# Seven products for eight: the feed-forward blocks of a decoder layer on one core, by Strassen's method

## The chip, the core and the metric

The kernel is written for one Trainium2 chip and runs on one of its cores, as a single program. The metric is the device time of one execution in microseconds (us), lower is better; several executions are timed and their median is given. One further execution was recorded by the hardware profiler; all views of the profile below are of that one. In them PE is TensorE (matmuls), PEld its weight loads, DVE VectorE, ACT ScalarE, POOL GpSimd, and SP the engine whose queue issues the transfers. L199 is line 199 of the kernel.

## What is computed

One decoder layer on 512 tokens of width 1024 in float32. The parts that the change touches are the two SwiGLU feed-forward blocks (FFNs), hidden width 2816, at the head of the layer and after the mixers:

```python
def swiglu(x, w_gate, w_up, w_down):
    return (jax.nn.silu(x @ w_gate) * (x @ w_up)) @ w_down

h = x + 0.5 * swiglu(rms_norm(h, g_ffn1), w_ffn1_gate, w_ffn1_up, w_ffn1_down)
u = rms_norm(h, g_mix);  z = u @ w_in        # convolution branch, q, k, v, gates
...                                          # conv module, dilated attention, merge
h = h + (g_a * y_conv + g_b * y_attn) @ w_mix_out
h = h + 0.5 * swiglu(rms_norm(h, g_ffn2), w_ffn2_gate, w_ffn2_up, w_ffn2_down)
h = h + sigmoid(rms_norm(h, g_ple) @ w_ple_gate) * (p @ w_ple_proj)
y = rms_norm(h, g_final)
```

## The kernel before

Activations lie transposed: a tile is 128 features by 512 tokens (`T`, 73 of them), so the width is KD = 8 tiles and the hidden width KF = 22. A product runs as three matmuls in a format that the tensor engine takes at full rate: every operand is split into a high part, which ACT rounds off with a copy, and a low part, the difference, which DVE (or POOL) subtracts. `mm3` (L198 to L201) multiplies high by high, high by low and low by high into one bank of PSUM. Activations are split by `split` (L209), weights by `split_one` (L161): ACT writes `wh` (L177), DVE writes `wl` (L182); for the slabs of the mixer named in `POOLED`, POOL writes `wl` in two halves (L180).

Weights arrive as slabs of 128 partitions by up to 1024 columns, in the order that `slab_order` writes out. `slab` (L186), called when PE comes to a slab, issues the loads up to three slabs ahead of the splits and the splits two slabs ahead of the use; RAW = 3 tiles hold slabs as loaded and SPLIT = 3 pairs hold them split. All loads go through the SP queue.

`ffn` (L338) loops over the 22 hidden row blocks: a unit of 24 matmuls of 512 columns for gate into bank `pg`, one for up into `pu`. Then DVE multiplies by the tokens' 1/rms (R), ACT takes silu, DVE multiplies, and the hidden tile is split. After that it loops over the 8 output blocks of down: 66 matmuls each into bank `pd`, then DVE adds half of it to the residual, and `into` (L389) splits the new residual for the next stage and adds its square to the next norm. In FFN 1 the 31 DVE steps that make the rotary tables (`tables`) are handed out two at a time by `background` between the units of down.

`begin` (L241) loads x and the first two slabs in pieces and splits them; `Norm.by_token` and `on_all` produce 1/rms while PE goes on with products that don't need it yet. The mixers follow (L463 on): gated convolution inputs, head slots of attention with the convolution in PSUM by DVE beside them, merge gates, output products. FFN 2 and the per-layer embedding end the layer; there PE runs matmuls of 256 columns, since the last stage is done in two halves of the tokens (`pg<-xsh,pgh`).

Of the kernel before, what the change touches and what calls it, by code (L numbers as in the profile page):

```python
# [38 lines left out]
C_M0, C_M1, C_M2, C_FREQ = 0, 256, 768, 1280  # L39
NCST = 1281  # L40
MAGIC = float(0x5F3759DF)

# 2 KiB tiles of activations
NT = 73
SLAB = 1024          # columns of a weight slab
# weight slabs in flight: as loaded, and split
RAW = 3
SPLIT = 3
AHEAD = 2            # slabs split ahead of their use
# slabs whose second part GpSimd takes, while VectorE works on the convolution in PSUM  # L50
POOLED = ("win", "v", "ao")
# steps of the depthwise convolution beside a unit of each kind
# [23 lines left out]

def slab_order():
    out = []
    for m in range(KF):
        out += [("g1", m), ("u1", m)]  # L80
    out += [("d1", m, j) for m in range(KD) for j in range(3)]
# [11 lines left out]
    for m in range(KF):  # L93
        out += [("g2", m), ("u2", m)]
    out += [("d2", m, j) for m in range(KD) for j in range(3)]
    out += [("pT",), ("pp", 0), ("pp", 1)]
    out += [("pg", m) for m in range(KD)]
    return out
# [3 lines left out]
def block_kernel(ctx: ExitStack, tc: tile.TileContext, a, out):  # L102
# [18 lines left out]
    def bank(n="ps"):  # L121
        return psum.tile([P, S], F32, name=name(n), tag="ps", bufs=6)
# [4 lines left out]
    # ---- weights: loaded ahead, split into two parts that the tensor engine takes exactly  # L127
    order = slab_order()
    state = {"load": 0, "split": 0, "use": 0}
    raws, halves = {}, {}  # L130

    def source(key):
        kind = key[0]
        if kind in ("d1", "d2"):
            lo, hi = ((0, 1024), (1024, 1920), (1920, 2816))[key[2]]
            return a["w_ffn%s_down" % kind[1]][key[1], :, lo:hi]
# [4 lines left out]
        n = {"g1": "w_ffn1_gate", "u1": "w_ffn1_up", "g2": "w_ffn2_gate", "u2": "w_ffn2_up", "win": "w_in",  # L141
             "ao": "w_attn_out", "co": "w_conv_out", "mx": "w_mix_out", "pg": "w_ple_gate", "pp": "w_ple_proj"}[kind]
        return a[n][key[1]]

    def raw_tile():
        return wts.tile([P, SLAB], F32, name=name("wr"), tag="wr", bufs=RAW)

    def split_tiles():
        return (wts.tile([P, SLAB], F32R, name=name("wh"), tag="wh", bufs=SPLIT),
                wts.tile([P, SLAB], F32R, name=name("wl"), tag="wl", bufs=SPLIT))  # L150

    def load_one():
        i = state["load"]
        src = source(order[i])
        w = src.shape[-1]
        r = raw_tile()
        nc.sync.dma_start(r[:, :w], src)
        raws[i] = (r, w)
        state["load"] = i + 1

    def split_one():  # L161
        i = state["split"]
        r, w = raws.pop(i)
        kind = order[i][0]
        if kind == "pg":
            hs, ls = [], []
            for c in range(2):
                z = r[:, c * S:(c + 1) * S]
                h, l = T("pgh", F32R), T("pgl", F32R)
# [5 lines left out]
        else:  # L175
            h, l = split_tiles()
            A.activation(h[:, :w], r[:, :w], AF.Copy)  # L177
# [3 lines left out]
            else:  # L181
                V.tensor_sub(l[:, :w], r[:, :w], h[:, :w].bitcast(F32))  # L182
            halves[i] = (h, l)
        state["split"] = i + 1

    def slab(key):  # L186
# [3 lines left out]
        while state["split"] <= min(i + AHEAD, len(order) - 1):  # L190
            while state["load"] <= state["split"]:
                load_one()
            split_one()
        while state["load"] < min(state["split"] + RAW, len(order)):
            load_one()
        return halves.pop(i)

    def mm3(ps, wh, wl, xh, xl, start, stop):  # L198
        PE.matmul(ps, wh, xh, start=start, stop=False)  # L199
        PE.matmul(ps, wh, xl, start=False, stop=False)  # L200
        PE.matmul(ps, wl, xh, start=False, stop=stop)  # L201

    def unit(ps, key, xs, start=True, stop=True, at=0):
        h, l = slab(key)
        for k, (xh, xl) in enumerate(xs):
            c = slice((at + k) * P, (at + k + 1) * P)
            mm3(ps, h[:, c], l[:, c], xh, xl, start and k == 0, stop and k == len(xs) - 1)
# [13 lines left out]
    # ---- constants, and the first loads  # L221
    gx = const.tile([P, V_DW + S], F32, name="gx")
    gains, x0 = gx[:, :V_DW], gx[:, V_DW:]
    taps = const.tile([P, KD * TAPS], F32, name="taps")
    ident = const.tile([P, P], F32, name="ident")
    cst = const.tile([P, NCST], F32, name="cst")
# [14 lines left out]
    def begin():  # L241
        """The first two slabs and x arrive in pieces, in the order in which they are used."""
        rs_ = [raw_tile() for _ in range(2)]
        hl = [split_tiles() for _ in range(2)]
        x = [x0] + [T("x") for _ in range(KD - 1)]
        xs = []
        cuts = [slice(0, 256), slice(256, 512), slice(512, 1024)]

        def piece(j):
            for i in range(2):  # L250
                nc.sync.dma_start(rs_[i][:, cuts[j]], source(order[i])[:, cuts[j]])

        def part(j):
            c = cuts[j]
            for i in range(2):
# [3 lines left out]
        nc.sync.dma_start(gx, a["gx"])  # L259
# [6 lines left out]
        state["load"] = state["split"] = 2  # L266
        load_one()
        nc.sync.dma_start(cst, a["cst"])
        nc.sync.dma_start(taps, a["taps"])
        for c in range(KD):  # L270
            xs.append(split(x[c], "xs", gain(V_G1, c)))
            if c in (0, 2, 3):
# [4 lines left out]
    class Norm:  # L277
        """The sum of squares over the features, and 1 / rms of every token: by token, and on every partition."""
# [58 lines left out]
    # ---- FFN  # L337
    def ffn(n, xs, norm, resid, after, first=False):  # L338
        R = None
        hid = []  # L340
        late = []

        def finish(pg, pu, tg, tu, gated=False):
            if not gated:
                V.tensor_mul(tg, pg, R)
                A.activation(tg, tg, AF.Silu)
            V.tensor_mul(tu, pu, R)
            V.tensor_mul(tu, tu, tg)  # L348
            hid.append(split(tu, "hid"))

        for m in range(KF):
            pg, pu = bank("pg"), bank("pu")
            tg, tu = T("tg"), T("tu")
            if first and m == 0:
                ga = slab(("g" + n, m))
                for t in resid:
                    norm.add(t)
                norm.flush()
                ua = slab(("u" + n, m))
                for k, (xh, xl) in enumerate(xs):  # L360
                    c = slice(k * P, (k + 1) * P)
                    mm3(pg, ga[0][:, c], ga[1][:, c], xh, xl, k == 0, k == KD - 1)
                    mm3(pu, ua[0][:, c], ua[1][:, c], xh, xl, k == 0, k == KD - 1)
                late.append((pg, pu, tg, tu))
                continue
            unit(pg, ("g" + n, m), xs)
            gated = R is not None
            if gated:
                V.tensor_mul(tg, pg, R)
                A.activation(tg, tg, AF.Silu)  # L370
            else:
                norm.by_token()
            unit(pu, ("u" + n, m), xs)
            if not gated:
                R = norm.on_all()
                for z in late:
                    finish(*z)
                late.clear()
            finish(pg, pu, tg, tu, gated)
        xs.clear()  # L380
        for m in range(KD):
            p = bank("pd")
            for j, (k0, k1) in enumerate(((0, 8), (8, 15), (15, 22))):
                unit(p, ("d" + n, m, j), hid[k0:k1], start=j == 0, stop=j == 2)
                background(2)
            V.scalar_tensor_tensor(resid[m], p, 0.5, resid[m], op0=OP.mult, op1=OP.add)
            after(m)

    def into(v, xs, norm, resid):  # L389
        def after(m):  # L390
# [529 lines left out]
```

## Time and profile before

| | |
|---|---|
| median of 3 runs | 1349.77 us (1349.27 to 1349.83) |
| span of the profiled execution | 1347.4 us |
| PE busy | 1334.2 us, 99% |
| DVE, ACT, POOL busy | 796.8, 499.7, 198.8 us |
| granted clock of TensorE, mean | 0.998 |
| bytes moved | 127.48 MB, 95 GB/s |

The profiled execution's own time beyond its span is not listed; the timed runs lie 1.9 to 2.4 us above the span. A row of a group gives line, engine, operation, what it writes and reads, shapes and count, then the sum busy, the mean duration in ns, and the idle time before it with what ended it. A row of the timeline gives start, duration, engine, line, operation and how many in a row are merged. A row of a stretch gives each engine's busy time, in brackets its instructions, then TensorE's granted clock, the share of the transfer engines and GB/s.

### The profile page before, as it was taken

How to read it: one execution, taken by the hardware profiler on the slowest of the kernel's cores; microseconds unless marked ns; L12 is line 12 of the kernel's file. 1: busy time of each engine (PE TensorE's matmuls, PEld its weight loads, DVE VectorE, ACT ScalarE, POOL GpSimd, SP SyncE). 2: the span in 40 equal slices, each digit the busy share in tenths (PEclk: the TensorE clock that was granted, in tenths of full speed). 3: DMA queues.
4: the chain of work that ended last, by engine and by line, in shares of the span. 5: the costliest groups of instructions: out<-in, count | busy, mean ns of one | idle time of the engine just before them, and what ended most of it. 6: DMA issues, size and time to landing. Idle time of an engine off the chain costs nothing.

```text
span 1347.4 us, 16023 instructions
## 1 busy us (share of the span) xinstructions
PE 1334.2 (99%) x6340; PEld 1127.7 (84%) x6340; DVE 796.8 (59%) x1283; ACT 499.7 (37%) x704; POOL 198.8 (15%) x164
## 2 busy tenths in 40 slices
PE   9999999999999999999999999999999999999997
PEld 7888888888888888989898878888888888888897
DVE  6544444455359887777778957555444444334465
ACT  5322332222332355555563345343222233223353
POOL 0000000000155443333334340000000000000020
PEclk9999999999999999999999999999999999999999
DMA  6222322333322222222222222222223222332321
GB/s 229 94 94 97 106 94 92 101 101 97 104 86 102 79 94 71 86 68 75 67 90 79 95 94 93 95 94 94 94 94 104 100 94 90 102 100 87 108 79 63
DMA packets 37947, 127.48 MB, mean 95 GB/s; under 512 B 4208, under 2 KB 4976, under 8 KB 37872
## 3 DMA queue, kind: packets, MB, share of 16 engines
q1 hardware_dynamic: 37872, 126.46, 27.9%
q8 instruction: 49, 0.80, 0.2%
q14 instruction: 26, 0.21, 0.0%
HBM read 124.35 MB, written 2.10 MB: 94 GB/s over the span
## 4 chain that ended last, share of the span: by engine, by line
PE 96%; DVE 3%; ACT 0%; DMA 0%; issue 0%; SPq 0%; DVEq 0%
PE pg L200 9%; PE pg L201 9%; PE pg L199 9%; PE pd L199 6%; PE pu L199 6%; PE pd L201 6%; PE pd L200 6%; PE pu L200 6%; PE pu L201 6%; PE pq L201 3%; PE pq L199 3%; PE pq L200 3%; PE pv L643 2%; PE pv L644 2%; PE pv L645 2%; PE pb L199 1%
## 5 line engine op out<-in xcount | busy, mean ns | idle before, releaser
L177 ACT ACTIVATE wh<-wr 128x1024 fp32r<-128x1024 f32 (+2 forms) x229 | 232.7, 1018 | 133.7 <-PE pd L200 55.5
L180 POOL TENSOR_TENSOR wl<-wr,wh 128x512 fp32r<-128x512 f32 (+1 forms) x152 | 187.6, 1257 | 621.2 <-ACT wh L177 606.2
L182 DVE TENSOR_TENSOR wl<-wr,wh 128x1024 fp32r<-128x1024 f32 x153 | 183.1, 1197 | 160.4 <-ACT wh L177 159.6
L199 PE MATMUL pg<-xsh,wh 128*128 128x512 f32 x480 | 188.6, 393 | 0.9 <-ACT xsh L217 0.9
L200 PE MATMUL pg<-xsl,wh 128*128 128x512 f32 x480 | 187.1, 390 | 0.3 <-DVE xsl L218 0.3
L201 PE MATMUL pg<-xsh,wl 128*128 128x512 f32 x480 | 187.0, 390 | 0.0
L483 DVE SCALAR_TENSOR_TENSOR acc<-glu,taps,acc 128x511 f32<-128x511 f32 (+14 forms) x240 | 165.0, 732 | 0.0
L199 PE MATMUL pu<-xsh,wh 128*128 128x512 f32 x352 | 137.2, 390 | 0.0
L201 PE MATMUL pu<-xsh,wl 128*128 128x512 f32 x352 | 137.0, 389 | 0.0
L200 PE MATMUL pu<-xsl,wh 128*128 128x512 f32 x352 | 137.0, 389 | 0.0
L199 PE MATMUL pd<-hidh,wh 128*128 128x512 f32 x352 | 136.9, 389 | 0.0
L200 PE MATMUL pd<-hidl,wh 128*128 128x512 f32 x352 | 136.9, 389 | 0.0
L201 PE MATMUL pd<-hidh,wl 128*128 128x512 f32 x352 | 136.9, 389 | 0.0
L199 PEld LDWEIGHTS pg<-xsh,wh 128*128 128x128 f32 x480 | 90.2, 188 | 20.7 <-ACT xsh L217 1.3
L200 PEld LDWEIGHTS pg<-xsl,wh 128*128 128x128 f32 x480 | 90.1, 188 | 20.0 <-DVE xsl L218 1.1
L201 PEld LDWEIGHTS pg<-xsh,wl 128*128 128x128 f32 x480 | 90.0, 188 | 18.9
L214 ACT ACTIVATE hidh<-tu 128x512 fp32r<-128x512 f32 x44 | 27.9, 633 | 188.3 <-DVE tu L348 188.3
L171 POOL TENSOR_TENSOR pgl<-wr,pgh 128x512 fp32r<-128x512 f32 x8 | 10.9, 1365 | 487.2 <-PE pp L201 467.2
L201 PEld LDWEIGHTS pu<-xsh,wl 128*128 128x128 f32 x352 | 66.1, 188 | 13.8
L201 PEld LDWEIGHTS pd<-hidh,wl 128*128 128x128 f32 x352 | 66.1, 188 | 13.8
L200 PEld LDWEIGHTS pu<-xsl,wh 128*128 128x128 f32 x352 | 66.1, 188 | 13.7
L200 PEld LDWEIGHTS pd<-hidl,wh 128*128 128x128 f32 x352 | 66.1, 188 | 13.7
(202 smaller groups left out, 2335.7 us busy)
## 6 DMA issues: line engine op xcount, KB each, us to landing
wr<-in_w_in SPq DMA_DIRECT2D x56, 512.0 KB, 3.2
wr<-in_w_ffn_gate SPq DMA_DIRECT2D x43, 512.0 KB, 3.2
wr<-in_w_ffn_up SPq DMA_DIRECT2D x43, 512.0 KB, 3.2
wr<-in_w_ffn_down SPq DMA_DIRECT2D x32, 448.0 KB, 3.3
wr<-in_w_ffn_down SPq DMA_DIRECT2D x16, 512.0 KB, 3.5
wr<-in_w_v SPq DMA_DIRECT2D x16, 384.0 KB, 2.9
wr<-in_w_conv_out SPq DMA_DIRECT2D x8, 512.0 KB, 3.2
wr<-in_w_mix_out SPq DMA_DIRECT2D x8, 512.0 KB, 3.2
```

Source lines behind the costliest of these rows:

```text
L171: (G if c else V).tensor_sub(l, z, h.bitcast(F32))
L177: A.activation(h[:, :w], r[:, :w], AF.Copy)
L180: G.tensor_sub(l[:, c:c + w // 2], r[:, c:c + w // 2], h[:, c:c + w // 2].bitcast(F32))
L182: V.tensor_sub(l[:, :w], r[:, :w], h[:, :w].bitcast(F32))
L199: PE.matmul(ps, wh, xh, start=start, stop=False)
L200: PE.matmul(ps, wh, xl, start=False, stop=False)
L201: PE.matmul(ps, wl, xh, start=False, stop=stop)
L214: A.activation(hh, src, AF.Copy)
L483: bg.append(lambda acc=acc, g=g, w=w, s=s: V.scalar_tensor_tensor(acc[:, s:], g[:, :S - s], w, acc[:, s:], op0=OP.mult, op1=OP.add))
L643: PE.matmul(pv[b][:, :384], xh, wh[:, c], start=first_, stop=False)
L644: PE.matmul(pv[b][:, :384], xh, wl[:, c], start=False, stop=False)
L645: PE.matmul(pv[b][:, :384], xl, wh[:, c], start=False, stop=last_)
```

## The change

Gate and up, and down, are computed by blocks of two by two: hidden row block m goes with m + 11, feature chunk c with c + 4 (for down, output block m with m + 4), and the 512 tokens are two halves of 256. The product of such a two-by-two weight block with a two-by-two activation block is made of seven products of half size (the variant with shared sums) instead of eight. PE multiplies with 256 columns of tokens.

- The first two pairs of row blocks (`EARLY`) are done whole, while the norm is formed; the others need activations that are already normalised (`normed`).
- Each step (`step`) of gate/up takes one pair of row blocks, both gate and up. Its four weight quarters (128 by 1024) are loaded as two transfers each. POOL makes four sums of quarters (`sum_one`), ACT all high parts, DVE six of the seven low parts and POOL that of T4.
- On the activations, `operands` makes four differences of 256 columns on POOL, then high parts on ACT and low parts on DVE.
- Results come out of three banks: ACT copies three products to SBUF, DVE adds the others to them or to their result; pieces of this work are queued (`job`) and handed out beside the products within budgets per engine (`work`).
- Down has four rounds over 3, 3, 2 and 3 pairs of hidden blocks (`ROUNDS`), each in two halves of the outputs, placed between the gate/up steps by `PLAN`. A round adds its results to the residual: DVE from PSUM, POOL from SBUF (in the last round DVE).
- Tiles are planned anew: 61 of `T`, 16 of 1024 columns (`W`) for weights as loaded, summed and split alike, and for some scores. The residual lies in one constant tile, masks are loaded after FFN 1, and wide scores take two tiles. The mixer's first gates come one unit later and the last products take the feature chunks in the order LAST.

```diff
+PRODUCTS = ("B11", "B21", "T2", "T1", "T3", "B22", "T4")
+EARLY = 2
+ROUNDS = ((0, 1, 2), (3, 4, 5), (6, 7), (8, 9, 10))
+PLAN = (("gu", 2), ("gu", 3), ("dn", 0, 0), ("dn", 0, 1), ("gu", 4), ("gu", 5), ("gu", 6), ("dn", 1, 0), ("dn", 1, 1),
+        ("gu", 7), ("gu", 8), ("gu", 9), ("dn", 2, 0), ("gu", 10), ("dn", 2, 1), ("dn", 3, 0), ("dn", 3, 1))
...
+    def sum_one():
...
+        if q == "B11":
+            r = z(A11)
+            mixed[k, 1] = W("s1")[:, :w]
+            G.tensor_add(mixed[k, 1], z(A21), z(A22))
+        elif q == "B21":
+            r = z(A12)
+            mixed[k, 2] = W("s2")[:, :w]
+            G.tensor_sub(mixed[k, 2], mixed[k, 1], z(A11))
+        elif q == "T2":
+            r = mixed[k, 2]
+            s3 = z(A21, True)
+            G.tensor_sub(s3, z(A11, True), s3)
+            mixed[k, 3] = s3
+        elif q == "T1":
+            r = mixed.pop((k, 1))
+            mixed[k, 4] = W("s4")[:, :w]
+            G.tensor_sub(mixed[k, 4], z(A12, True), mixed.pop((k, 2)))
...
     def split_one():
...
+            A.activation(h, r, AF.Copy)
+            (G if q == "T4" else V).tensor_sub(l, r, h.bitcast(F32))
...
     def slab(key):
...
+        more, sums = (1, 1) if key[0] == "gq" else (MORE, SUMS)
+        for j in range(i + 1, i + AHEAD + sums + 1):
+            ahead("load", load_one, j + 1)
+            ahead("sum", sum_one, j + 1)
+            ahead("split", split_one, min(j, i + AHEAD) + 1)
...
+    def operands(x1, x2, t12, t34):
...
+                A.activation(h, src, AF.Copy)
+                V.tensor_sub(l, src, h.bitcast(F32))
...
+        def sub(o, p_, q_):
+            return lambda: G.tensor_sub(o, p_, q_), 0, 0, 0.7
+        todo = {"T1": sub(t12[:, lo], x1[:, hi], x1[:, lo]), "T3": sub(t34[:, lo], x2[:, hi], x1[:, hi]),
+                "T2": sub(t12[:, hi], x2[:, hi], t12[:, lo]), "T4": sub(t34[:, hi], x2[:, lo], t12[:, hi]),
...
+    def step(n, key, ts, fin, *most, n_bg=0):
+        pa, pe, pd = bank("pa"), bank("pe"), bank("pd")
+        into_ = {"B11": pa, "B21": pe, "T2": pa, "T1": pd, "T3": pa, "B22": pd, "T4": pa}
...
+        for q in PRODUCTS:
+            h, l = slab((n, key, q))
+            ps = into_[q]
+            for i in range(k):
+                th, tl = ts[i][q]
+                for g in range(2):
+                    c = slice((g * k + i) * P, (g * k + i + 1) * P)
+                    mm3(ps[:, g * 256:(g + 1) * 256], h[:, c], l[:, c], th, tl,
+                        q in ("B11", "B21", "T1") and i == g == 0, i == k - 1, True)
+            work(*most)
+            background(n_bg)
+            if q in ("B11", "T2", "T1"):
+                t = kept[q] = T("p")
+                A.activation(t, ps, AF.Copy)
+            else:
+                z, old = {"B21": ((0, 0), "B11"), "T3": ((1, 1), "T1"), "B22": ((0, 1), "T2"), "T4": ((1, 0), None)}[q]
+                fin(*z, kept.get(old), ps)
...
+        def gate_up(j):
...
+                V.tensor_add(t, t, ps)
...
+                job(lambda: A.activation(t[:, lo], t[:, lo], AF.Silu), 0.4)
+                job(lambda: V.scalar_tensor_tensor(dst, t[:, hi], 0.5, t[:, lo], op0=OP.mult, op1=OP.mult), v=0.4)
+            step(n, ("gu", j), xn, out, *((1.0, 0.9, 3) if j < 4 else (0.9, 0.9, 3)), n_bg={4: 2, 5: 1, 6: 2}.get(j, 0))
...
+        def down(r, half):
...
+                add(V, a_, b_, ps)
...
+                elif not last:
+                    for z in rest:
+                        job(lambda z=z: add(G, *z), g=1.3)
...
+            step(n, ("dn", r, half), [ops[j] for j in ROUNDS[r]], out, *((1.3, 1.4, 2) if last else (0.7, 0.7, 2)), n_bg=1)
```

More of the change, by code (lines that the diff above doesn't have):

```diff
@@ L74, with ffn_order @@
 ROUND = 12582912.0
+def ffn_order(n):
+    out = [("gq", n, j, q) for j in range(EARLY) for q in range(4)]
+    for step in PLAN:
+        out += [(n, step, q) for q in PRODUCTS]
+    return out
 def slab_order():
     out = []
-    for m in range(KF):
-        out += [("g1", m), ("u1", m)]
-    out += [("d1", m, j) for m in range(KD) for j in range(3)]
+    out += ffn_order("1")
     for c in range(KD):
@@ L92, in slab_order @@
     out += [("mx", m) for m in range(KD)]
-    for m in range(KF):
-        out += [("g2", m), ("u2", m)]
-    out += [("d2", m, j) for m in range(KD) for j in range(3)]
+    out += ffn_order("2")
     out += [("pT",), ("pp", 0), ("pp", 1)]
@@ L128, in block_kernel, with quarter @@
     order = slab_order()
-    state = {"load": 0, "split": 0, "use": 0}
+    state = {"load": 0, "sum": 0, "split": 0, "use": 0}
     raws, halves = {}, {}
+    def quarter(n, step, q):
+        x_, y = divmod(q, 2)
+        if step[0] == "gu":
+            m = step[1] + x_ * KF // 2
+            return [a["w_ffn%s_%s" % (n, g)][m][:, y * S:(y + 1) * S] for g in ("gate", "up")]
+        js = ROUNDS[step[1]]
+        c = y * KF // 2 + js[0]
+        m = 4 * x_ + 2 * step[2]
+        return [a["w_ffn%s_down" % n][m + i][:, c * P:(c + len(js)) * P] for i in range(2)]
     def source(key):
         kind = key[0]
-        if kind in ("d1", "d2"):
-            lo, hi = ((0, 1024), (1024, 1920), (1920, 2816))[key[2]]
-            return a["w_ffn%s_down" % kind[1]][key[1], :, lo:hi]
         if kind == "v":
@@ L152, in load_one @@
+    quarters, mixed = {}, {}
     def load_one():
         i = state["load"]
[L154 to L158, printed above, removed]
-        state["load"] = i + 1
+        key = order[i]
+        q = product(key)
+        if key[0] == "gq":
+            raws[i] = fetch(*quarter(key[1], ("gu", key[2]), key[3]))
+        elif q is None:
+            raws[i] = fetch(source(key))
+        elif q == "B11":
+            for z in (A21, A22, A11):
+                quarters[key[:2], z] = fetch(*quarter(key[0], key[1], z))
+        elif q == "B21":
+            quarters[key[:2], A12] = fetch(*quarter(key[0], key[1], A12))
+        state["load"] = i + 1
@@ L161, in split_one @@
     def split_one():
         i = state["split"]
[L163 to L166, printed above, removed]
+        r, q, kind = raws.pop(i), product(order[i]), order[i][0]
+        if q is not None:
+            w = r.shape[-1]
+            h, l = W("wh", F32R)[:, :w], W("wl", F32R)[:, :w]
+            A.activation(h, r, AF.Copy)
+            (G if q == "T4" else V).tensor_sub(l, r, h.bitcast(F32))
+            halves[i] = h, l
+        elif kind == "pg":
+            hs, ls, low = [], [], W("wl", F32R)
@@ L167, in split_one @@
             for c in range(2):
                 z = r[:, c * S:(c + 1) * S]
-                h, l = T("pgh", F32R), T("pgl", F32R)
+                h, l = T("pgh", F32R), low[:, c * S:(c + 1) * S]
                 A.activation(h, z, AF.Copy)
@@ L181, in split_one, with ahead @@
             else:
-                V.tensor_sub(l[:, :w], r[:, :w], h[:, :w].bitcast(F32))
+                V.tensor_sub(l, r, h.bitcast(F32))
             halves[i] = (h, l)
         state["split"] = i + 1
+    def ahead(what, one, to):
+        while state[what] < min(to, len(order)):
+            one()
     def slab(key):
@@ L189, in slab, with mm3, unit @@
         state["use"] = i + 1
[L190 to L195, printed above, removed]
-        return halves.pop(i)
[L198 to L203, printed above, removed]
-        h, l = slab(key)
-        for k, (xh, xl) in enumerate(xs):
-            c = slice((at + k) * P, (at + k + 1) * P)
-            mm3(ps, h[:, c], l[:, c], xh, xl, start and k == 0, stop and k == len(xs) - 1)
+        more, sums = (1, 1) if key[0] == "gq" else (MORE, SUMS)
[3 more added lines that the diff above has]
+            ahead("split", split_one, min(j, i + AHEAD) + 1)
+        ahead("load", load_one, i + AHEAD + RAW + 1)
+        if product(order[min(i + AHEAD + RAW, len(order) - 1)]):
+            ahead("load", load_one, i + AHEAD + RAW + more + 1)
+        return halves.pop(i)
+    def mm3(ps, wh, wl, xh, xl, start, stop, part=False):
+        PE.matmul(ps, wh, xh, start=start, stop=False, skip_group_check=part)
+        PE.matmul(ps, wh, xl, start=False, stop=False, skip_group_check=part)
+        PE.matmul(ps, wl, xh, start=False, stop=stop, skip_group_check=part)
+    def unit(ps, key, xs, ks=range(KD), beside={}):
+        h, l = slab(key)
+        for k in ks:
+            if k in beside:
+                beside[k]()
+            c = slice(k * P, (k + 1) * P)
+            mm3(ps, h[:, c], l[:, c], xs[k][0], xs[k][1], k == ks[0], k == ks[-1])
     def split(src, n, scale=None, w=S):
@@ L335, in on_all @@
             return R
[L338 to L352, printed above, removed]
-            tg, tu = T("tg"), T("tu")
[L354 to L357, printed above, removed]
-                norm.flush()
[L359 to L387, printed above, removed]
@@ L389, in into, with job, work @@
-    def into(v, xs, norm, resid):
-        def after(m):
-            xs.append(split(resid[m], "xs", gain(v, m)))
-            norm.add(resid[m])
-            if m == KD - 1:
-                norm.flush()
-        return after
+    jobs = []
+    def job(f, a_=0.0, v=0.0, g=0.0):
+        jobs.append((f, (a_, v, g)))
+    def work(*most):
+        sum_ = [0.0] * 3
+        while jobs:
+            sum_ = [x_ + y for x_, y in zip(sum_, jobs[0][1])]
+            if any(x_ > y for x_, y in zip(sum_, most)):
+                break
+            jobs.pop(0)[0]()
@@ L397, in block_kernel, with into, first_, second @@
+    def into(v, xs, norm, resid):
+        seen = []
+        def first_(m):
+            xs[m] = split(resid[m], "xs", gain(v, m))
+        def second(m):
+            norm.add(resid[m])
+            seen.append(m)
+            if len(seen) == KD:
+                norm.flush()
+        return first_, second
     bg = []
@@ L451, in tables @@
         bg.append(end)
-    x, xs = begin()
     norm = Norm()
+    x, xs = begin(norm)
+    norm.flush()
     h = x
-    us, unorm = [], Norm()
-    nxt = into(V_GM, us, unorm, h)
-    def after1(m):
-        nxt(m)
-        if m == 0:
-            tables()
-    ffn("1", xs, norm, h, after1, first=True)
+    us, unorm = [None] * KD, Norm()
+    ffn("1", xs, norm, h, into(V_GM, us, unorm, h))
     background(len(bg))
+    masks = []
+    for g in range(NG):
+        masks.append(T("mask"))
+        nc.sync.dma_start(masks[g][:, :C_M[g + 1] - C_M[g]], a["cst"][:, C_M[g]:C_M[g + 1]])
     conv = {}
```

330 lines of the change are left out of this document (259 added, 71 removed).

## The prediction, made before the changed kernel ran

> **What bounds the kernel now.** I read the page first: span, busy shares, then the chain that ended last.
>
> ```profile
> span 1347.4 us, 16023 instructions
> PE 1334.2 (99%) x6340; PEld 1127.7 (84%) x6340; DVE 796.8 (59%) x1283; ACT 499.7 (37%) x704; POOL 198.8 (15%) x164
> PE 96%; DVE 3%; ACT 0%; DMA 0%; issue 0%; SPq 0%; DVEq 0%
> ```
>
> The chain is 96% PE, so the time is the sum of the matmuls' spacings plus a few gaps. A matmul's listed duration (390 ns for 512 columns) overlaps its neighbours, so I take spacings from the timeline: where both feed-forward blocks (FFNs) begin and end, and a stretch of 256-column matmuls in the last stage, whose form is the one that the change uses.
>
> ```profile
> 4.87 0.50 PE L199 MATMUL pg<-xsh,wh 128*128 128x512 f32 x1
> 368.03 0.39 PE L199 MATMUL pb<-xsh,wh 128*128 128x512 f32 x1
> ...
> 911.35 0.39 PE L199 MATMUL pg<-xsh,wh 128*128 128x512 f32 x1
> ...
> 916.95 0.79 PE ss L307 x8
> 923.35 0.86 PE R L328 x2
> ...
> 1272.26 0.39 PE L199 MATMUL pp<-wh,wh 128*128 128x512 f32 x1
> ...
> 1326.96 0.28 PE L200 MATMUL pg<-xsl,pgh 128*128 128x256 f32 x1
> 1334.99 0.28 PE L201 MATMUL pg<-xsh,pgl 128*128 128x256 f32 x1
> ```
>
> FFN 1 takes 363.2 us (368.03 - 4.87), FFN 2 360.9 (1272.26 - 911.35). Each holds 1584 matmuls of 512 columns (22 x 16 x 3 for gate and up, 8 x 22 x 3 for down); less the 1.65 us of norm work in FFN 2 (ss and R), that is 0.227 us each. The 256-column stretch holds 67 spacings in 8.03 us: 0.120 us each. So half a matmul costs 0.53 of a whole one, with its own weight load each time.
>
> Next the view by stretches, one from inside FFN 2, for who is free beside PE.
>
> ```profile
> core 0: us, PE busy (x) PEld busy (x) DVE busy (x) ACT busy (x) POOL busy (x), PEclk, DMA share, GB/s
> 1000.00:1100.00 100.00, 100.00 (x443) 82.78 (x442) 48.36 (x56) 28.64 (x37) 0.00 (x0) 1.00 0.29 100
> ```
>
> In the FFNs POOL does nothing today, DVE half, ACT under a third. That is the room that the change's additions go into, so its prices matter.
>
> ```profile
> L182 DVE TENSOR_TENSOR wl<-wr,wh 128x1024 fp32r<-128x1024 f32 x67 | 82.1, 1226 | 65.2 <-ACT wh L177 64.6
> L215 DVE TENSOR_TENSOR hidl<-tu,hidh 128x512 fp32r<-128x512 f32 x44 | 30.4, 692 | 30.8 <-ACT hidh L214 30.8
> L218 DVE SCALAR_TENSOR_TENSOR xsl<-x,gx,xsh 128x512 fp32r<-128x512 f32 x28 | 20.8, 751 | 18.5 <-ACT xsh L217 18.4
> L810 DVE TENSOR_TENSOR gt<-gt,x 128x256 f32<-128x256 f32 x14 | 6.0, 426 | 0.5
> L711 DVE TENSOR_TENSOR sg<-pg,R 128x512 f32<-128x512 f32 x16 | 11.0, 687 | 13.7 <-PE pg L201 13.7
> L180 POOL TENSOR_TENSOR wl<-wr,wh 128x384 fp32r<-128x384 f32 x32 | 31.6, 1014 | 50.8 <-ACT wh L177 50.8
> 388.85 1.29 POOL L180 TENSOR_TENSOR wl<-wr,wh 128x512 fp32r<-128x512 f32 x1 [1.14 <-ACT wh L177]
> L177 ACT ACTIVATE wh<-wr 128x1024 fp32r<-128x1024 f32 x181 | 189.6, 1048 | 82.7 <-issue 38.8 <-PE pa L200 20.1 <-PE pb L200 13.9
> L214 ACT ACTIVATE hidh<-tu 128x512 fp32r<-128x512 f32 x44 | 27.9, 633 | 188.3 <-DVE tu L348 188.3
> L803 ACT ACTIVATE gt<-gt 128x256 f32<-128x256 f32 x16 | 6.7, 417 | 15.7 <-DVE gt L802 15.5
> L768 ACT ACTIVATE pp<-pp 128x512 f32<-128x512 f32 x8 | 4.5, 592 | 3.0 <-PE pp L201 3.0
> L415 DVE TENSOR_SCALAR n<-n 128x512 f32<-128x512 f32 x3 | 1.3, 423 | 0.0
> ```
>
> POOL: 1.014 us for 384 columns, 1.29 for 512, so 2.16 ns a column; estimated 0.74 for 256, 1.84 for 768, 2.40 for 1024. DVE: 0.69 for 512, 1.226 for 1024; 0.43 for 256, 0.96 for 768.
>
> The rows that decide are a place where both work on SBUF at once, the mixer's start:
>
> ```profile
> 384.17 0.68 DVE L518 TENSOR_TENSOR cos<-cos,R 128x512 f32<-128x512 f32 x1
> 384.77 1.78 DVE L519 TENSOR_TENSOR sin<-sin,R 128x512 f32<-128x512 f32 x1
> 384.55 3.15 POOL L180 TENSOR_TENSOR wl<-wr,wh 128x512 fp32r<-128x512 f32 x2 [7.29 <-ACT wh L177]
> 374.86 1.18 DVE L315 TENSOR_SCALAR y<-t 128x4 int32<-128x4 int32 x1
> 374.72 2.54 POOL L180 TENSOR_TENSOR wl<-wr,wh 128x512 fp32r<-128x512 f32 x2 [0.46 <-ACT wh L177]
> ```
>
> A 0.68 us product becomes 1.78, two POOL subtractions 3.15 instead of 2.54, and even four columns of DVE wait 1.18 for POOL. They exclude each other: L518 ends at 384.85, L519 at 386.55, and one POOL subtraction lies between, then POOL ends at 387.70. So DVE and POOL together need 1.70 a pair, against 1.29 + 0.69 = 1.98 end to end: start-up overlaps, 0.14 per instruction, and the exclusive hold is the duration less 0.14. POOL holds 0.60, 1.15, 1.70, 2.26 us for 256, 512, 768, 1024 columns; DVE, with both inputs in SBUF, 0.28, 0.55, 0.82, 1.09 (L218's form 0.61). With one input in PSUM it isn't concerned: L711 keeps 687 ns as a mean though POOL works beside part of it.
>
> The Trainium skill, "SBUF — State Buffer", section "Who interferes with whom", speaks against the change: the pair of ports that VectorE and GpSimd share is an exclusive lock for the whole instruction, and a VectorE instruction with two SBUF inputs contends with a GpSimd one that reads SBUF. By that rule the sum below is 1423; by shared bandwidth it would be PE's 1302.
>
> **The change part by part.** *Matmuls.* Per FFN the first 4 of 22 row blocks stay whole (192 matmuls, 43.6 us). Nine gate/up steps take 7 products x 4 x 2 x 3 = 168 half matmuls each: 20.16 us, against 96 whole ones, 21.8. Down has 8 steps, 7 x k x 2 x 3 with k = 3 (six) or 2 (two): 15.1 and 10.1 us, against 16.3 and 10.9. Sum 43.6 + 181.4 + 110.9 = 335.9, against 1584 x 0.227 = 359.6: PE alone gains 23.7 us per FFN.
>
> The Trainium skill, "TensorE: Matmul & The Clock Gate", section "Back-to-back issue gap", has N/2.4 + 2.5 ns isolated, 109 and 216 for 256 and 512; by it the gain would be 34 per FFN. The measured 120 and 227 decide.
>
> *Shared SBUF work, gate/up step.* Added on POOL: 4 sums of 1024 columns, one low part (product T4), 4 operand differences of 256: 5 x 2.26 + 4 x 0.60 = 13.7. On DVE: 6 low parts (7.36 alone, 6 x 1.09), operand low parts 0.28 + 3 x 0.55, gating 3 x 0.28: 9.3. Together 23.0 us of one resource, beside PE's 20.16 and the old 21.8. DVE's PSUM additions (3 x 0.69 and 0.43) can lie beside POOL.
>
> *Down.* k = 3: POOL 5 x 1.70 + 3 residual additions of 1.15, DVE 6 x 0.82: 16.9 beside 15.1. k = 2: 8 x 1.15 + 6 x 0.55 = 12.5 beside 10.1. Last round: 8.5 + 4.9, 3 additions (1.65) and the next norm's 4 splits and 4 sums (4.6): 19.7 beside 15.1.
>
> *Early part* (beside 43.6 of PE): 4 + 2 sets of operands (2.4 on POOL, 1.93 on DVE) 26.0, 8 normalised inputs 4.9, 4 gatings 2.2, 8 low parts 8.7: 41.8.
>
> Sum: 9 x 23.0 + 4 x 16.9 + 2 x 12.5 + 2 x 19.7 + 41.8 = 381 us of exclusive holds per FFN, over PE's 336 and over the 361 to 363 of today. About 394 such instructions are counted; end to end, without overlapped starts, it is 381 + 394 x 0.14 = 436. I take a quarter of the way, 395: in the alternating rows the overlap is there, but DVE's queue also stands behind PE (a result's addition waits for its product, and the next low part is queued behind it) and behind ACT's high part, and then nobody holds the ports.
>
> *Rotary tables*, 31 DVE steps of FFN 1: free today with POOL idle, now under the same lock; 18 have two SBUF inputs, 18 x 0.55 = 9.9, the others (0.42 each) between 0 and 5: +12. *Start:* squares go between the x splits on ACT, 8 x (0.72 + 0.62) and the slab pieces, some 3 us later than PE could go; bounds 0 and +5. *Spill:* the last splits and sums and the first slabs' low parts lie outside the FFN: -4 each, bounds 0 and -9.
>
> *Loads.* Per gate/up step 8 transfers of 256 KB instead of 4 of 512; bytes are equal.
>
> ```profile
> 5.44 3.03 SPq L262 DMA_DIRECT2D x<-in_xT  x4
> x<-in_xT SPq DMA_DIRECT2D x7, 256.0 KB, 5.0
> cst<-in_cst SPq DMA_DIRECT2D x1, 640.5 KB, 6.4
> L285 ACT ACTIVATE sq<-x 128x512 f32<-128x512 f32 x28 | 16.7, 617 | 0.0
> L217 ACT ACTIVATE xsh<-x,gx 128x512 fp32r<-128x512 f32 x28 | 20.1, 724 | 90.2 <-DVE x L386 65.7 <-DVE x L748 22.7 <-DMA x<-in_xT 1.7
> ```
>
> Issue is 0.76 us each here, 6 of 20 us of the queue; landing 5.0 us, while a quarter is asked for some four products (11 us) before its sum. I cost it at nothing, covered by that lead; gone, it is up to 5 us per step. *ACT* per gate/up step: 7 x 1.05 + 3 copies, 4 silu halves and operand highs, some 13 of 20 us; hidden. *Banks:* bank `pa` takes B11, T2, T3 and T4, and each waits until ACT's copy or DVE's addition of the one before has read it; one other product lies between (2.88 us, 1.44 at k = 2) against 0.59 or 0.69: nothing if those engines come in time; if not, all of PE stands behind. *Masks:* their 640 KB go to the queue after FFN 1, ahead of later slabs, 6.4 us against a lead of five slabs (27 us): nothing. *Other mixer edits* (scores in two tiles, the first gates later, order of the last k): between -2 and +3, taken as 0; PE covers them as before.
>
> Total: FFN 2 395 - 4 - 360.9 = +30; FFN 1 395 + 12 + 3 - 4 - 363.2 = +43. 1347.4 + 73 = 1420.4 of span; the median 1349.77 lies 2.4 above the span, so 1423 us. Lower end: 381 - 9 each, tables 10: +11 and +19, 1380. Upper end: 436 each, no spill, 12 + 5: +75 and +90, 1515.
>
> **The rivals.**
> *PE stays the bound (faster).* Each engine alone has room (ACT 13, DVE 13.6, POOL 15.0 of 20.16 us in a step), the jobs are handed out in small budgets, and 1024 columns on POOL are an extrapolation. It decides in the gate/up step: if the holds fall from 23.0 under 21.8, which takes 0.24 us off each of the five 2.26 us holds, the loss is gone; under 20.16 all of PE's gain arrives: 1349.8 - 2 x 23.7 = 1302. For it: whole-queue figures. Against: the rows at 384 us. Between: 1302 to 1347.
> *Waits in order.* A low part waits for the copy and high part on ACT and then POOL's hold: 0.59 + 1.05 + 2.26 + 1.09 = 5.0 us before a product may start, against two products of lead, 5.8; at k = 2 it is 0.59 + 0.63 + 1.15 + 0.55 = 2.9 against 2.9. If these chains bind everywhere, holds run end to end: 1490 to 1515.
> *No change.* Gains of PE and losses to the ports cancel, 1347 to 1353; it needs holds of 360 per FFN.
>
> **How the numbers follow.** Ports bind, 1380 to 1490: 0.72; PE bound, faster: 0.18; waits on top: 0.07; no change: 0.03. Forecast 1423, the first case's. Some 0.2% (2.7 us) is what a measurement can tell from no change. The likeliest case's own range is 1380 to 1490; for 8 in 10 the low end reaches into PE's case, to 1325. Slower 0.72 + 0.07, same 0.03, faster 0.18.
>
> **What would show it.** In the stretches of the FFNs: POOL and DVE busy nearly all the time, 1024-wide DVE low parts of 2 to 3 us instead of 1.226 and 1024-wide POOL sums over 2.4; in PE's waits, matmuls waiting for low parts from DVE or POOL, one or two us at a time; gate/up steps of 23 to 25 us. Matmul spacing at 0.120 with no waits, and steps of 20.2 us, would prove me wrong, as would POOL sums of 1024 columns well under 2.2 us.

## The result: 1500.9 us against 1349.8, and the profile after

The changed kernel took 1500.9 us (median of 4 runs, 1500.41 to 1503.7), before 1349.8: 1.1122 times as long, with an interval of 1.1106 to 1.1138. The direction was forecast; the time lies 78 us above the forecast and 11 above the stated range. The page of the changed kernel, the lines that answer to the first fence of the prediction:

```profile
span 1498.7 us, 21967 instructions
PE 1345.9 (90%) x8428; PEld 1222.3 (82%) x8428; DVE 1246.7 (83%) x1541; ACT 676.9 (45%) x1048; POOL 825.3 (55%) x490
PE 50%; DVE 27%; issue 8%; POOL 7%; ACT 6%; DMA 1%; SPq 0%; DVEq 0%; POOLq 0%; ACTq 0%
```

PE is on half of the chain that ended last, where it was 96%. Where the FFNs begin and end, from the timeline, and a run of products in a step of FFN 1:

```profile
5.34 0.50 PE L291 MATMUL pg<-xsh,wh 128*128 128x512 f32 x1
445.03 0.40 PE L291 MATMUL pb<-xsh,wh 128*128 128x512 f32 x1
...
995.87 0.39 PE L291 MATMUL pg<-xsh,wh 128*128 128x512 f32 x1
1412.40 0.40 PE L291 MATMUL pp<-wh,wh 128*128 128x512 f32 x1
...
294.28 0.28 PE L291 MATMUL pa<-bh,wh 128*128 128x256 f32 x1
302.80 0.28 PE L293 MATMUL pa<-bh,wl 128*128 128x256 f32 x1
```

FFN 1 takes 439.7 us (363.2 before), FFN 2 416.5 (360.9), the mixers between 550.8 (543.3) and all that follows FFN 2 86.3 (75.1): +77, +56, +8 and +11 us make the 151 of the span. The last two rows stand 71 spacings apart: 0.120 us, so where PE is fed the half matmuls cost what they should. The stretches that hold the steps of the two FFNs (columns as in the prediction's view):

```profile
core 0: us, PE busy (x) PEld busy (x) DVE busy (x) ACT busy (x) POOL busy (x), PEclk, DMA share, GB/s
59.40:445.00 385.60, 319.65 (x2436) 309.83 (x2437) 356.70 (x297) 173.20 (x266) 292.40 (x149) 0.94 0.25 81
1047.00:1412.40 365.40, 313.18 (x2436) 303.86 (x2437) 339.83 (x264) 172.69 (x264) 294.55 (x146) 0.96 0.26 85
```

2436 half matmuls need 292 us; the steps take 386 and 365. DVE is busy 93% of that, POOL 76 to 81%, and "busy" includes standing before the ports, as the groups of the two engines show (mean in ns):

```profile
L248 DVE TENSOR_TENSOR wl<-s,wh 128x1024 fp32r<-128x1024 f32 x54 | 112.9, 2093 | 13.3 <-ACT wh L247 13.3
L248 DVE TENSOR_TENSOR wl<-wr,wh 128x1024 fp32r<-128x1024 f32 x54 | 105.7, 1961 | 20.7 <-ACT wh L247 20.7
L585 DVE TENSOR_TENSOR p<-p,pa 128x512 f32<-128x512 f32 x18 | 12.2, 678 | 4.6 <-PE pa L293 4.3 <-ACT tg L527 0.2
L219 POOL TENSOR_TENSOR s<-wr,wr 128x1024 f32<-128x1024 f32 x18 | 53.8, 2987 | 23.6 <-PE pe L292 20.9 <-DVE wl L248 2.6
L248 POOL TENSOR_TENSOR wl<-wr,wh 128x1024 fp32r<-128x1024 f32 x18 | 53.2, 2954 | 19.5 <-ACT wh L247 16.1 <-DVE wl L248 3.4
```

The same DVE subtraction that took 1226 ns takes 1961 and 2093; POOL's 1024 columns, estimated at 2.40 us, take 2.95 to 2.99; the addition with one input in PSUM (L585) stays at 678, near the 687 of L711 before. And who made PE wait (us in total, times, longest):

```profile
PE pa L293 <- DVE wl L248: 39.4, 18, 7.6
PE pd L293 <- DVE wl L248: 25.4, 25, 3.1
PE pa L291 <- DVE p L585: 17.4, 9, 6.1
PE pe L293 <- DVE wl L248: 9.3, 14, 1.2
PE pa L293 <- POOL wl L248: 6.8, 4, 2.4
```

PE waits for DVE's low parts above all (74 us in these rows), seldom for POOL's.

### The profile page after: what moved, and what is told of

It reads as the page before. It is cut to its first block, busy times and chain, and to the rows that moved or that the text cites. A ratio compares the mean times of both kernels' runs of the same rounds, so it can differ in the third digit from the quotient of the medians.

```text
span 1498.7 us, 21967 instructions
## 1 busy us (share of the span) xinstructions
PE 1345.9 (90%) x8428; PEld 1222.3 (82%) x8428; DVE 1246.7 (83%) x1541; ACT 676.9 (45%) x1048; POOL 825.3 (55%) x490
## 4 chain that ended last, share of the span: by engine, by line
PE 50%; DVE 27%; issue 8%; POOL 7%; ACT 6%; DMA 1%; SPq 0%; DVEq 0%; POOLq 0%; ACTq 0%
DVE wl L248 11%; DVE bl L464 4%; PE pa L291 3%; PE pa L293 3%; PE pg L293 3%; PE pg L292 3%; PE pg L291 3%; PE pa L292 3%; PE pq L292 3%; PE pq L293 3%; PE pq L291 3%; DVE gx L610 3%; ACT wh L247 3%; POOL t L469 2%; POOL wl L248 2%
## 5 line engine op out<-in xcount | busy, mean ns | idle before, releaser
L293 PE MATMUL pa<-bh,wl 128*128 128x256 f32 x696 | 204.9, 294 | 31.3 <-DVE wl L248 24.5
L291 PE MATMUL pa<-bh,wh 128*128 128x256 f32 x696 | 204.6, 294 | 29.5 <-DVE p L585 17.4
L292 PE MATMUL pa<-bl,wh 128*128 128x256 f32 x696 | 202.7, 291 | 2.3 <-DVE bl L464 2.3
L248 DVE TENSOR_TENSOR wl<-s,wh 128x1024 fp32r<-128x1024 f32 (+2 forms) x102 | 182.2, 1789 | 18.3 <-ACT wh L247 16.4
L248 DVE TENSOR_TENSOR wl<-wr,wh 128x1024 fp32r<-128x1024 f32 (+2 forms) x102 | 175.6, 1723 | 25.2 <-ACT wh L247 25.2
L293 PEld LDWEIGHTS pa<-bh,wl 128*128 128x128 f32 x696 | 139.1, 200 | 35.6 <-DVE wl L248 27.8
L291 PEld LDWEIGHTS pa<-bh,wh 128*128 128x128 f32 x696 | 138.7, 199 | 33.9 <-issue 22.5
L293 PE MATMUL pd<-bh,wl 128*128 128x256 f32 x464 | 137.0, 295 | 25.5 <-DVE wl L248 25.4
L292 PEld LDWEIGHTS pa<-bl,wh 128*128 128x128 f32 x696 | 139.0, 200 | 2.7 <-DVE bl L464 2.7
L291 PE MATMUL pd<-bh,wh 128*128 128x256 f32 x464 | 134.0, 289 | 5.4 <-ACT p L501 5.4
```

Of the source, the lines that this page charges most:

```text
L248: (G if q == "T4" else V).tensor_sub(l, r, h.bitcast(F32))
L291: PE.matmul(ps, wh, xh, start=start, stop=False, skip_group_check=part)
L292: PE.matmul(ps, wh, xl, start=False, stop=False, skip_group_check=part)
L293: PE.matmul(ps, wl, xh, start=False, stop=stop, skip_group_check=part)
```

## The experiments

Theories: P, the port pair that DVE and POOL exclude each other from binds, by the sum of the holds; D, DVE alone is overloaded and POOL relieves it; C, products start late since low parts come only two products ahead. Q and R came up on the way.

**All of POOL's work in the FFNs to DVE** (e1). In `sum_one`, T4's low part, `operands` and the residual additions:

```diff
-            G.tensor_add(mixed[k, 1], z(A21), z(A22))
+            V.tensor_add(mixed[k, 1], z(A21), z(A22))
...
-            (G if q == "T4" else V).tensor_sub(l, r, h.bitcast(F32))
+            V.tensor_sub(l, r, h.bitcast(F32))
...
-            return lambda: G.tensor_sub(o, p_, q_), 0, 0, 0.7
+            return lambda: V.tensor_sub(o, p_, q_), 0, 0, 0.7
...
-                        job(lambda z=z: add(G, *z), g=1.3)
+                        job(lambda z=z: add(V, *z), g=1.3)
```

> All that POOL does in the feed-forward blocks (four sums of weight quarters, T4's low part, operand differences, residual additions) goes to DVE; POOL is empty there. Theory P (the port pair that DVE and POOL exclude each other from is what binds): the holds shrink to DVE's own stream, 191 us alone + 50 us with one PSUM input + 129 us taken over = 370 us a block alone, some 330 to 350 with overlapped starts, so each block falls from 440 and 416 us to 350 to 375, and the time from 1500.9 to 1350 to 1420 us. Theory D (DVE is simply overloaded and POOL relieves it): about 100 us more per block, near 1700 us. Theory C (products start late since low parts are made only two products ahead, whoever makes them): no fall, 1490 or more.

Measured 1393.6 us, 1.032 of before (1.029 to 1.035), 107 us less than the change as it was. Groups and the two stretches of steps:

```profile
L248 DVE TENSOR_TENSOR wl<-wr,wh 128x1024 fp32r<-128x1024 f32 x72 | 87.8, 1219 | 6.1 <-ACT wh L247 6.1
L248 DVE TENSOR_TENSOR wl<-s,wh 128x1024 fp32r<-128x1024 f32 x54 | 65.9, 1221 | 11.9 <-ACT wh L247 11.3
56.00:385.70 329.70, 305.46 (x2436) 300.82 (x2437) 312.80 (x442) 174.16 (x266) 5.11 (x4) 0.97 0.30 97
985.50:1302.50 317.00, 304.63 (x2437) 301.61 (x2438) 294.98 (x409) 173.21 (x264) 0.00 (x0) 0.97 0.31 97
```

DVE does 145 instructions more a block and is busy 44 us less. D and C fall. DVE is busy 313 of 330 us in the steps of block 1 (FFN 1) and 295 of 317 in block 2 (FFN 2), PE 305 in both: neither has much room left, and which of the two sets the time where wasn't taken apart.

**The sums left out** (e2).

```diff
-            mixed[k, 1] = W("s1")[:, :w]
-            G.tensor_add(mixed[k, 1], z(A21), z(A22))
+            mixed[k, 1] = z(A21)
```

and the like for the other three; the results are then no longer the layer's.

> The four sums of weight quarters of every step are left out; the products take the quarters themselves, so seven products of the same size run with other weights. Everything else stays, on POOL too. Theory P: the holds of a gate/up step fall from 23.0 to 14.0 us, under PE's 20.2, so the blocks come to 345 to 365 us each and the time to 1340 to 1390 us. Theory D: POOL's sums cost DVE nothing, so within 20 us of 1500.9. Theory C: the low parts still come two products ahead, so 1470 to 1500 us.

Measured 1351.9 us, 1.0016 (1.0005 to 1.0027).

```profile
58.40:362.70 304.30, 298.69 (x2436) 296.94 (x2437) 242.87 (x296) 173.31 (x267) 123.61 (x81) 0.98 0.31 99
963.20:1261.80 298.60, 295.93 (x2436) 295.10 (x2437) 217.04 (x263) 171.69 (x264) 116.69 (x79) 0.99 0.31 100
```

The steps fall to 304 and 299 us, PE's 292 and 12 and 6 more: PE binds, as P has it. With seven products at PE's own pace the kernel is as fast as before, not 47 us faster: the FFNs' early parts take 53 and 50 us where 44 were priced, and the stages behind them keep their +7 and +11.

**T4's low part alone to DVE** (e3); the one line of e1.

> One piece alone: T4's low part goes from POOL to DVE, 17 instructions a block. Theory P: 2.26 us of hold become 1.09 (1.70 to 0.82, 1.15 to 0.55), 17 us a block, so some 30 to 35 us less, 1465 to 1472 us. Theory D: DVE gets 18 us more a block, 1520 to 1537 us. Theory C: unchanged, 1495 to 1505 us.

Measured 1500.1 us (1.1109, 1.1065 to 1.1153): nothing, where P said 30 less. It is what C said of this run; but C's figures for e1 and e2, and for e4 below, are missed by 80 us and more. **The sums alone to DVE** (e4); the four lines of e1.

> The four sums alone go from POOL to DVE; T4's low part, the operand differences and the residual additions stay on POOL. Theory P: holds fall by 4.7 us a gate/up step, 3.5 and 2.4 a down step, 68 us a block, to some 313 us, under PE's 336; 345 to 375 us a block, 1350 to 1420 us in all. Theory D: 73 us more DVE work a block, about 1640 us. Theory C: unchanged, 1490 or more.

Measured 1409.6 us (1.0438, 1.0408 to 1.0469), as P has it. To see what became of e3's 17 us I took the instructions of the steps one by one: an instruction's own work is the duration of its shape while the other engine is quiet (DVE 0.42, 0.69, 0.95, 1.22 us, POOL 0.74, 1.29, 1.84, 2.39 for 256, 512, 768, 1024 columns), the rest is waiting at the ports. Block 1, us:

| kernel | steps | DVE own | DVE waits | DVE other (PSUM etc.) | POOL own | POOL waits |
|---|---|---|---|---|---|---|
| changed | 386 | 170 | 144 | 60 | 231 | 66 |
| e3, T4 low on DVE | 383 | 188 | 126 | 58 | 197 | 63 |
| e9, T4 low left out | 372 | 170 | 124 | 58 | 195 | 57 |
| e5, quarter pieces | 388 | 170 | 79 | 58 | 268 | 113 |
| e7, half pieces | 382 | 170 | 110 | 59 | 247 | 96 |
| e4, sums on DVE | 338 | 240 | 50 | 54 | 95 | 44 |
| e1, all on DVE | 330 | 292 | 2 | 52 | 5 | 2 |
| e2, no sums | 304 | 170 | 36 | 55 | 94 | 32 |

The figures are good to some 3 us. Instructions overlap at their starts, so a row can add up to more than the steps. (The expectations of e5 and e7 have 10 us less own work and 10 more waits for POOL: there its 18 residual additions stand at the price of 256 columns, though each has two rows of 256.)

In e3 DVE's own work grew by 18 us and its waits fell by 18. That gave theory Q: DVE's queue with its waits binds, not the sum of holds.

**POOL's sums in quarter pieces** (e5). The last pair of lines is repeated in kind for the other three sums and for T4's low part:

```diff
+    def fine(f, o, p_, q_):
+        for c in range(0, o.shape[-1], 256):
+            f(o[:, c:c + 256], p_[:, c:c + 256], q_[:, c:c + 256])
...
-            G.tensor_add(mixed[k, 1], z(A21), z(A22))
+            fine(G.tensor_add, mixed[k, 1], z(A21), z(A22))
```

> POOL's sums of quarters and T4's low part are issued in pieces of 256 columns, four for one of 1024; the same elements, the same engines. Theory P (the sum of exclusive holds binds): 4 x 0.60 us instead of 2.26, so no gain, 1495 to 1515 us. Theory Q (what binds is DVE's own queue, in which every subtraction with two SBUF inputs stands behind the POOL instruction in progress: in the steps of block 1 of the changed kernel 170 us of own work, 144 us of such waits and 60 us of other work make 357 of 386 us): a wait is at most 0.6 us instead of 2.26, the waits fall to 50 to 90 us, and the time to 1440 to 1480 us; the sum of holds, 350 us a block, stays as a floor under the steps.

Measured 1516.7 us (1.1241, 1.1218 to 1.1263), 2 us over what P allowed. DVE's waits fell by 65 us as Q had it and the time did not; the queue that is full is now POOL's:

```profile
59.80:447.80 388.00, 329.28 (x2436) 317.75 (x2437) 290.85 (x297) 173.32 (x266) 367.85 (x349) 0.93 0.25 80
L204 POOL TENSOR_TENSOR s<-wr,wr 128x256 f32<-128x256 f32 x116 | 142.2, 1253 | 12.3 <-PE pe L299 12.3
L255 DVE TENSOR_TENSOR wl<-s,wh 128x1024 fp32r<-128x1024 f32 x54 | 85.6, 1587 | 22.5 <-ACT wh L251 22.5
```

Q falls as it stood; R says that the longer of the two queues, with its waits, sets the steps. **Half pieces** (e7), `w = o.shape[-1] // 2` in place of 256:

> POOL's sums and T4's low part in two pieces each. Theory R: the port pair makes each of the two queues wait for the other, and the longer queue, own work with its waits, sets the steps. Whole pieces left DVE the longer one (in block 1 of the changed kernel 170 + 144 + 60 us on DVE, 221 + 76 on POOL, of 386), quarter pieces POOL (258 + 123 on POOL, 170 + 79 + 58 on DVE, of 388); halves lie between, both at 320 to 355, so the steps take 345 to 370 us and the time is 1430 to 1480 us, under both. Theory P (the sum of holds alone): 1495 to 1515, as with whole and quarter pieces.

Measured 1491.0 us (1.1048, 1.1016 to 1.1080): 10 less than whole pieces, 25 less than quarters, so an optimum lies between, but the gain is far smaller than R had it, and P's 1495 is missed by 4.

```profile
59.40:441.90 382.50, 322.90 (x2437) 313.85 (x2438) 322.87 (x297) 173.40 (x267) 334.33 (x232) 0.93 0.26 82
PE pa L301 <- POOL wl L205: 31.1, 24, 4.0
PE pa L301 <- DVE wl L256: 19.3, 14, 4.1
```

Neither queue is full, yet the steps are nearly as long: PE's waits are shared between the low part from POOL and those from DVE. Three ways of cutting the same work give 382 to 388 us in block 1 and 360 to 379 in block 2. That is near P: the pair acts as one resource, and cutting mostly moves the waits from one queue to the other. Counted from the instructions of e7, one that needs the pair is in progress in 370 of the 382 us of block 1 and in 356 of the 360 of block 2.

**T4's low part left out** (e9).

```diff
+            if q == "T4":
+                l = h
```

> T4's low part is left out: the product takes the high part twice, so PE does the same matmuls and POOL 17 subtractions a block fewer; DVE's own work is as in the changed kernel. Theory P (sum of holds): 9 x 2.26 + 6 x 1.70 + 2 x 1.15 = 33 us of hold a block go, some 1435 us. Theory R' (the pair is the resource, but what is late first is DVE's queue, in which a POOL instruction costs what DVE waits for it, 144 us for 148 of them): 17 x 1.0 us a block, some 1465 us; it would also say why T4's low part on DVE moved nothing, 18 us of own work for 17 us of waits. If T4's low part plays no role wherever it is made: 1495 to 1503 us.

Measured 1473.5 us (1.0917, 1.0885 to 1.0948): 27 us less, nearest to R' (1465) and less than half of what the sum of holds says. DVE's waits fell by 20 us in block 1 and POOL got idle time instead. So an instruction taken off POOL was worth the wait that it caused on DVE, some 1 us, not its hold of 2.26, as long as DVE's queue is what is late first; moved to DVE it costs the 1.1 us that it saves. This is a reading of the table that fits e3 and e9, not one that a run tried. It doesn't say why half pieces bring so little: there, by the count above, the pair itself was full.

**Seven products for gate and up alone, all on DVE** (e6). Built on e1; down is whole again, in the same four rounds, and its hidden tiles are split whole, without operand differences:

```diff
+            for at in range(4):
+                m = 4 * (at // 2) + 2 * half + at % 2
+                h, l = slab(("dn", n, ("dn", r, half), at))
+                p = bank("pd")
...
+                        mm3(p, h[:, c], l[:, c], ops[j][y][0], ops[j][y][1], first_, end_)
...
+                V.tensor_add(resid[m], resid[m], p)
```

> Seven products for gate and up alone, down whole in the same four rounds (each output block adds its part to the residual from PSUM), and all sums and low parts on DVE, POOL empty in the blocks. Theories P and Q: DVE needs 18.6 us of a gate/up step's 20.2 and 6.6 of 16.3 in a down step, so PE binds again: 43.6 + 181.4 + 119.9 = 345 us a block plus 5 to 10 at its start, 350 to 355 against 361 to 363 before; the block's end is light for DVE, so the stages behind it lose less than 5 us; 1325 to 1345 us. Theory C (products wait for low parts made only two products ahead, however light the queues): the gate/up steps stay 10% over 20.2 us, 1365 us or more.

Measured 1340.8 us, 0.9937 of before (0.9921 to 0.9954): faster than both kernels, and where it was expected.

```profile
5.30:363.60 358.30, 349.55 (x2242) 317.78 (x2243) 276.80 (x387) 163.42 (x244) 5.08 (x4) 1.00 0.35 115
908.80:1261.30 352.50, 347.65 (x2244) 318.03 (x2243) 253.71 (x339) 154.16 (x225) 0.00 (x0) 1.00 0.31 100
```

FFN 2 takes 352.5 us (360.9 before), with PE busy 99% and DVE 72%; the mixers take 545.2 and what follows FFN 2 77.1, each 2 us over before. **The same with POOL making the sums and T4's low part** (e8):

> Seven products for gate and up alone and down whole, with POOL making the four sums and T4's low part of each gate/up step, in 1024 columns as in the changed kernel. DVE's own work is 12.4 us a step, the holds add to 19.8 beside PE's 20.2. Theories P and R: sharing the ports costs nothing as long as neither queue fills: DVE's waits for five POOL instructions are 5 to 7 us, so 17 to 20 us a step and 1340 to 1365 us. If any work on POOL beside DVE's low parts costs time, whatever the load: the 5 x 2.26 us a step come on top, some 1400 to 1440 us.

Measured 1365.0 us (1.0114, 1.0085 to 1.0143), the upper end of what was expected, 24 us over e6. Stretches as for e6 (PE only), and DVE's group:

```profile
5.30:380.00 374.70, 356.07 (x2243) 0.98 0.34 109
925.70:1285.00 359.30, 350.61 (x2244) 0.99 0.31 98
L253 DVE TENSOR_TENSOR wl<-wr,wh 128x1024 fp32r<-128x1024 f32 x54 | 91.5, 1696 | 1.2 <-ACT wh L252 1.2
```

With less than PE's time to do, the pair still costs something, though not the 5 x 2.26 us a step. Of the 24 us, 8 lie in the two early parts and 16 in the steps, 13 of those in FFN 1, which has the tables too; PE's longest waits there are 4.8 us for a low part from DVE and 4.0 for a high part from ACT.

## Why the prediction was right and wrong, point by point

*PE's gain.* Right: 0.120 us a half matmul, 292 us of steps a block; e2, where PE binds, comes to 304 and 299.

*The ports.* Right as mechanism, and the estimates extrapolated to 1024 columns too: POOL alone 2.40 us (the shortest in e2; estimated 2.40), DVE 1.22. The Trainium skill, "SBUF — State Buffer", section "Who interferes with whom", has VectorE and GpSimd locked out of each other; the traces agree: 1219 ns for DVE's low part with POOL empty (e1), 1961 to 2093 beside it. The rival by which PE stays the bound fell with the result, and e1 and e4 show that most of the loss hangs on what POOL does.

*The size.* The span came out 78 us over the forecast: 33 of them in the steps (21 in FFN 1, 12 in FFN 2), 18 in the two early parts, 27 at the edges behind the FFNs. The step that failed is the one between 381 us of holds and 436 end to end, where a quarter of the way was taken. Without the 42 us priced for the early part that left some 353 us for the steps of FFN 2, and with the tables 365 for FFN 1; they took 365 and 386. The holds themselves were nearly right. Counted from the trace's instructions by the prediction's prices they add up to 354 us in the steps of FFN 1 and 341 in FFN 2, end to end 405 and 389, so half to six tenths of the way was due. The quarter was to cover starts that don't overlap and times in which nobody holds the ports. Of the first kind there were 11 and 9 us (an instruction that needs the pair is in progress during 365 and 350 us), of the second 21 and 16: in 15 and 9 DVE works alone on instructions without two inputs in SBUF, and in 5 and 7 neither works. The sum's own upper end, 1515, covers the result; the range stopped at 1490, where "waits in order" begins.

A sum of holds was also the wrong instrument for one piece: e3 (0 for 31 expected) and e9 (27 for 65). In e9 the pair is in use 30 us less a block, as was to be expected, but the steps get only 14 and 18 us shorter; the rest became time of the second kind.

*Early part.* Priced at 43.6 us of PE with 41.8 of holds beside it, and 3 more in FFN 1; the sum took the 41.8, less than PE's own time. It took 54.0 and 51.2 until the first step, and the first product of that step stood another 10. The holds fit beside PE as a sum, but the timeline shows a chain: DVE's normalised input, POOL's difference, ACT's high part, DVE's low part. Before the first step:

```profile
45.57 1.41 DVE L534 SCALAR_TENSOR_TENSOR xn<-gx,R 128x512 f32<-128x512 f32 x2
46.39 2.12 POOL L469 TENSOR_TENSOR t<-xn 128x256 f32<-128x256 f32 x1 [6.51 <-DVE xn L534]
49.17 1.54 POOL L469 TENSOR_TENSOR t<-xn,t 128x256 f32<-128x256 f32 x2
49.93 0.63 ACT L463 ACTIVATE bh<-t 128x512 fp32r<-128x512 f32 x1 [5.51 <-POOL t L469]
50.60 0.69 DVE L464 TENSOR_TENSOR bl<-t,bh 128x512 fp32r<-128x512 f32 x1 [2.69 <-ACT bh L463]
```

That this chain is the cause was read, not tried by itself, and it isn't all. With nothing on POOL there (e6) the early parts still take 50.5 and 47.3 us; with the differences on POOL but no sums (e4) 54.3 and 51.5, with the sums but no differences (e8) 54.5 and 51.2. Either kind of work on POOL goes with some 4 us, and 4 to 7 us over PE's 43.6 stay open.

*Edges.* The mixer edits were taken as 0, and "spill" as a gain of 4 a block. It is a loss of 8 and 11 us: after the last product DVE still has additions, splits and norm sums to do, and the next stage waits for them:

```profile
1411.09 0.68 DVE L610 TENSOR_TENSOR gx<-gx,p 128x512 f32<-128x512 f32 x1
1414.14 1.41 DVE L312 SCALAR_TENSOR_TENSOR xsl<-gx,xsh 128x512 fp32r<-128x512 f32 x2
1418.27 3.87 DVE L390 TENSOR_TENSOR sq<-sq,sq 128x512 f32<-128x512 f32 x5
1422.05 2.29 DVE L268 TENSOR_TENSOR wl<-wr,wh 128x1024 fp32r<-128x1024 f32 x1
```

The low part of the next stage's slab (L268) stands behind all that; PE begins that stage at 1412.40. In e6 and e8, whose down is light for DVE, the edges shrink to 2 each.

*The rivals' prices.* 1302 us for "PE stays the bound" was too low: e2 is that case and takes 1351.9, since early parts, edges and the 12 and 6 us of the steps give back what PE gains. The time measured lies among those of "waits in order", but leads of two products alone don't make it: e2 and e6 have the same leads, and there PE binds. In both POOL's sums, a link of the rival's chain, are gone from POOL too; a longer lead with POOL's work left in place was not tried, so part of the rival stands open.

## What to carry to other kernels

Before work is moved to an idle POOL, add up what it holds against DVE's instructions with two inputs in SBUF: here some 244 us of POOL's work a block (by its durations alone) cost 107 us of time over both blocks, which DVE, 1.8 to 2 times as fast alone, gave back by doing the work itself. A removed instruction wasn't worth its own length in e3 and e9, rather the wait that it caused on the queue that was late. And a saving on the bound engine has to pay for its start and its end as well, which here took all of it until only gate and up were left.

## What the runs showed of the hardware that was not expected

After a wait of 7.6 us PE came back at little more than half its rate. The first product of the first step, from the chain that ended last:

```profile
64.07 3.37 DVE wl L248
...
71.69 0.21 PE pa L293
71.90 0.21 PE pa L291
72.12 0.21 PE pa L292
```

That is 0.213 us a half matmul instead of 0.120; the granted clock reads 0.50 from 64.0 to 71.6 us. Over the steps that makes a granted clock of 0.94 and 0.96 over the steps, 0.92 in places (e3), against 1.00 before. The Trainium skill, "TensorE: Matmul & The Clock Gate", section "What's actually happening", lets the gate fall to 4 of 8 pulses after an idle window; the trace agrees with the half rate. How much of the time that cost was not measured by itself. PE was busy 633 us in the steps of both blocks, 38 more than in e2, which has as many products; but in block 1 of the changed kernel DVE stood idle for PE's products only 1.6 us and POOL 16 of 386, so little of it held up these two directly.
